# First mixer: the whole convolution on VectorE, its normalized half multiplied into the output before the recurrence's half

## The chip, the cores and the metric

The kernel runs on one core of one Trainium2 chip. The core has TensorE (matrix products; PE in a profile), VectorE (DVE), ScalarE (ACT), GpSimd (POOL) and the DMA queues, most of whose transfers SyncE (SP) issues. The metric is device time in microseconds (us) of one execution, lower is better; three runs of the kernel before gave 2468.09, 2470.43 and 2472.05 us.

## The reference, cut to what matters

Two transformer blocks of 512 tokens and width 1024 run one after the other; the change is in the first mixer of the first block:

```python
h = x @ w_in                                   # 512 x 3072
q, f_pre, i_v, g, a, a_gate = split(h)         # each 512 x 512
f = lb + (1 - lb) * sigmoid(f_pre); k = (1 - lb) * sigmoid(-f_pre)
o = hgrn2_chunked(q, k, i_v, log(f))           # S_t = diag(f_t) S_{t-1} + k_t v_t^T, chunks of 32
o = o * rsqrt(mean(o * o) + eps)               # per head of 128
o = o * hg_norm_g * silu(g)
u = a * sigmoid(a_gate)
u = conv_causal(u, cv_w, 31 taps, per channel) + cv_b
u = silu(layer_norm(u, cv_ln_g, cv_ln_b))
y = concatenate([o, u]) @ w_out                # rows 0..511 of w_out meet o, 512..1023 meet u
x = layer_norm(ALPHA * x + y)                  # goes on into the cross attention
```

Everything is float32.

## The kernel before, in words

A float32 product is made of three TensorE products of split operands: `split` (L152, L153) writes a rounded high part with ScalarE and the remainder with VectorE, and `mm3` (L180 to L182) multiplies high by high, high by low and low by high. Weights come in units of two k-slices of 128 rows (`chunk`): a DMA into a ring of 5 buffers `raw`, then the two split instructions into a ring of 4 buffers `w` (the second half of an output projection, `wb`, has buffers of its own). A unit can be split only when the products of the unit four places earlier have been done.

The mixer makes, in the order of its code: the gate and the value of the convolution (`u`, with channels on partitions, four groups f of 128 channels by 512 tokens); the forget gate and `v`; the convolution (`conv`, L674 to L686: 31 lags, each one instruction per channel group, which adds a shifted copy of `u` times a tap to `acc`); the cumulative sums of the gates (`cums`); the product for q; keys and values of the coming cross attention from the memory (`kv_k`, `kv_v`); the recurrence (`recur`, four turns t of 128 tokens: `advance` transposes q and k (L415), multiplies them (L731), masks (L734), makes the state increments of four chunks (L742) and adds them up on VectorE (L749); `readout` multiplies them out head by head (L766, L769) and normalizes); the product for g; the transposes of the recurrence's result into `yT`; and the output projection `lin_out`, which runs the four k-slices of the recurrence's half first, then `conv_norm` (the convolution's transposes L556, its normalization and transposes into the other half of `yT`), then the rest.

Of the four channel groups of the convolution, three are VectorE's. For the fourth, each lag is an activation on ScalarE (L683, `u` times the tap into one buffer `conv`) and an addition on GpSimd (L684).

The framework sets the order: it simulates the program and writes one fixed list of instructions for each engine, by priorities which follow the order of the code, except that weight units are pulled ahead (`high_priority`, `ahead`) and that the convolution is pushed back by 3000 (`later`). So an instruction of each engine waits behind all that stand before it in its list, whether it needs them or not.

Of the kernel before, what the change touches and what calls it, by code (L numbers as in the profile page):

```python
# [13 lines left out]
AF = mybir.ActivationFunctionType  # L14
ALU = mybir.AluOpType
# [57 lines left out]
class Net:  # L73
# [284 lines left out]
        out(1, 0, x)  # L358
        yield

    def lin_out(self, xT, W, first, norm, nxt, k0=0, nk=8, between=None, aside=None):
        split = 4 if between else 0
        ua = self.chunk(W, 0, 512, k0, nk)
        ps = [None] * 4
        if between:
            for t in range(4):
                ps[t] = self.bank([128, 512])
                self.mm_b(ps[t:t + 1], [t], xT, ua, range(split), nk)
            between()
        ub = self.chunk(W, 512, 512, k0, nk, big=True)  # L370
        if aside:
            aside()
        nxt = nxt()
        nxt, early = nxt if isinstance(nxt, tuple) else (nxt, None)
        ev = self.tail(512, first, norm, nxt)
        for half, t in ((0, 0), (0, 1), (1, 0), (1, 1), (0, 2), (0, 3), (1, 2), (1, 3)):
            if half == 0:
                p = ps[t] or self.bank([128, 512])
                self.mm_b([p], [t], xT, ua, range(split, nk), nk)
                self.resid(t, p, 0, first)  # L380
                if early:
                    early(t)
            else:
                p = self.bank([128, 512])
                self.mm_b([p], [t], xT, ub, range(nk), nk)
                ev(t, p)

    def mm_b(self, ps, tiles, xT, units, ks, nk):
        for k in ks:
            u = units[k // 2]  # L390
            xh, xl = xT(k)
            for i, t in enumerate(tiles):
                tk = slice(t * 128, t * 128 + 128)
                self.mm3(ps[i], xh[:, tk], xl[:, tk], u[:, 0, k % 2], u[:, 1, k % 2], k == 0, k == nk - 1)

    def lin_b(self, xT, W, c0, evac, w=512, k0=0, nk=8, groups=((0, 1, 2, 3),), **kw):
        units = self.chunk(W, c0, w, k0, nk, **kw)
# [61 lines left out]
    def hgrn_mixer(self):  # L459
        nc, a = self.nc, self.a  # L460
        W = a["ab_w_in"][0]
        hi, lo = self.new_xT()
        for t in range(4):
            for half in range(2):
                self.to_T(self.r[t][:, half * 512:half * 512 + 512], hi, lo, t, half)
        xT = self.pair_view(hi, lo)

        pack1 = self.slot([128, 4, 512], name="pack1")
        pack2 = self.slot([128, 4, 512], name="pack2")
        lb, om, hg, cg = (pack1[:, i, :] for i in range(4))  # L470
        cb = pack2[:, 2, :]
        cw, cwT = pack2[:, 3, 0:128], pack2[:, 3, 128:256]
        nc.gpsimd.dma_start(cw[0:124, :], a["cv_w"][0, :, 0, :].rearrange("j (c p) -> (j c) p", p=128))
        nc.gpsimd.dma_start(cw[124:128, :], a["cv_b"][0].rearrange("(c p) -> c p", p=128))
        cps = self.xbank([128, 128])
        nc.tensor.transpose(cps, cw, self.ident)
        nc.scalar.activation(cwT, cps, AF.Copy)

        u = self.slot([128, 4, 512], name="u")
        acc = self.slot([128, 4, 512], name="acc")  # L480

        def ev_gate(f, ps, t0, t1):
            nc.scalar.activation(u[:, f, t0:t1], ps, AF.Sigmoid)

        def ev_a(f, ps, t0, t1):
            nc.vector.tensor_tensor(u[:, f, t0:t1], u[:, f, t0:t1], ps, ALU.mult)

        self.lin_a(xT, W, 2560, ev_gate, halves=True, units=self.first)
        self.lin_a(xT, W, 2048, ev_a)
        mT = self.mem_T(0)  # L490

        lbr = self.slot([128, 3, 512], name="lbr")
        nc.gpsimd.dma_start(lbr, a["lb_param"].unsqueeze(0).broadcast_to([128, 3, 512]))
        nc.vector.tensor_tensor(om, lbr[:, 0], lbr[:, 1], ALU.max)
        nc.vector.tensor_tensor(om, om, lbr[:, 2], ALU.max)
        for i in range(3):
            nc.vector.tensor_tensor(lbr[:, i], lbr[:, i], om, ALU.subtract)
        nc.scalar.activation(lbr, lbr, AF.Exp)
        nc.vector.tensor_tensor(om, lbr[:, 0], lbr[:, 1], ALU.add)
        nc.vector.tensor_tensor(om, om, lbr[:, 2], ALU.add)  # L500
        nc.vector.reciprocal(om, om)
        nc.vector.tensor_tensor(lb, lbr[:, 0], om, ALU.mult)
        nc.vector.tensor_scalar(om, lb, -1.0, 1.0, ALU.mult, ALU.add)

        lf = self.slot([128, 4, 512], name="lf")
        kt = self.slot([128, 4, 512], name="kt")
        ke = self.slot([128, 4, 512], name="ke")

        def ev_f(t, ps):
            nc.scalar.activation(lf[:, t], ps, AF.Sigmoid)  # L510
            nc.scalar.activation(kt[:, t], ps, AF.Sigmoid, scale=-1.0)
            nc.vector.tensor_tensor(lf[:, t], lf[:, t], om, ALU.mult)
            nc.vector.tensor_tensor(lf[:, t], lf[:, t], lb, ALU.add)
            nc.vector.tensor_tensor(kt[:, t], kt[:, t], om, ALU.mult)

        self.lin_b(xT, W, 512, ev_f)
        v = self.slot([128, 4, 512], name="v")
        self.lin_b(xT, W, 1024, lambda t, ps: nc.scalar.activation(v[:, t], ps, AF.Copy))
        nc.scalar.activation(lf, lf, AF.Ln)

        with self.later(3000):
            self.conv(u, acc, cwT)

        qt = self.slot([128, 4, 512], name="qt")
        dec = pack2[:, 3, 256:320].rearrange("p (t h c) -> p t h c", t=4, h=4)
        for t in range(4):
            self.cums(t, lf[:, t], kt[:, t], ke[:, t], qt[:, t], dec[:, t], TRI, REV, 32)

        self.lin_b(xT, W, 0, lambda t, ps: nc.vector.tensor_tensor(qt[:, t], qt[:, t], ps, ALU.mult))
        self.kv_k(0, mT)  # L530
        self.kv_v(0, mT)
        g = self.slot([128, 4, 512], name="g")
        self.bload(hg, a["hg_norm_g"][0])

        def ev_g(t, ps):
            nc.scalar.activation(g[:, t], ps, AF.Silu)
            nc.gpsimd.tensor_tensor(g[:, t], g[:, t], hg, ALU.mult)

        self.masked = [pack2[:, i, :].rearrange("p (h t) -> p h t", h=4) for i in range(2)]
        nc.gpsimd.memset(pack2[:, 0:2, :], 0.0)  # L540
        col = lambda x: lambda t, h: x[:, t, h * 128:h * 128 + 128]
        self.recur(qt, kt, ke, col(v), dec, TRI, 32, 128, col(qt))
        self.lin_b(xT, W, 1536, ev_g, ahead=700)
        yh, yl = self.new_xT("yT")
        for t in range(4):
            nc.gpsimd.tensor_tensor(qt[:, t], qt[:, t], g[:, t], ALU.mult)
            self.to_T(qt[:, t, :], yh, yl, t, 0)

        self.bload(cg, a["cv_ln_g"][0])
        self.bload(cb, a["cv_ln_b"][0])  # L550

        def conv_norm():
            for t in range(4):
                ps = self.xbank([128, 4, 128])
                for f in range(4):
                    nc.tensor.transpose(ps[:, f, :], acc[:, f, t * 128:t * 128 + 128], self.ident)  # L556
                pf = ps.rearrange("p a b -> p (a b)")
                mv, rs = self.ln_stats([pf])
                cu = self.tmp()
                nc.vector.scalar_tensor_tensor(cu, pf, mv[:, 0:1], cg, ALU.subtract, ALU.mult)  # L560
                nc.vector.scalar_tensor_tensor(cu, cu, rs[:, 0:1], cb, ALU.mult, ALU.add)
                nc.scalar.activation(cu, cu, AF.Silu)
                self.to_T(cu, yh, yl, t, 1)

        lg, lb_ = self.gains("ln_mix", 0)
        yT = self.pair_view(yh, yl)
        Wo = a["ab_w_out"][0]
        self.lin_out(yT, Wo, True, (lg, lb_), self.next_split, between=conv_norm)

    def gains(self, name, l):  # L570
        return self.bcast(self.a[name + "_g"][l], "w4k", 1024), self.bcast(self.a[name + "_b"][l], "w4k", 1024)
# [100 lines left out]
    def conv(self, u, acc, cwT):  # L672
        nc = self.nc
        for lag in range(31):  # L674
            for f in range(4):
                col = cwT[:, 4 * (30 - lag) + f:4 * (30 - lag) + f + 1]
                bias = cwT[:, 124 + f:125 + f]
                src, dst = u[:, f, :512 - lag], acc[:, f, lag:]
                if lag == 0:
                    (nc.gpsimd if f == 3 else nc.vector).tensor_scalar(dst, src, col, bias, ALU.mult, ALU.add)  # L680
                elif f == 3:
                    p = self.wt([128, 512], "conv", bufs=1)[:, lag:]
                    nc.scalar.activation(p, src, AF.Identity, scale=col)  # L683
                    nc.gpsimd.tensor_tensor(dst, dst, p, ALU.add)  # L684
                else:
                    nc.vector.scalar_tensor_tensor(dst, src, col, dst, ALU.mult, ALU.add)  # L686

# [611 lines left out]
```

## Time and profile before

| what | value |
|---|---|
| median of 3 runs | 2470.43 us (2468.09 to 2472.05) |
| the profiled execution | 2471.44 us, of which the span 2469.6 us |
| PE busy | 2414.4 us (98%) |
| DVE busy | 1509.4 us (61%) |
| ACT busy | 1024.4 us (41%) |
| POOL busy | 180.5 us (7%) |
| mean granted clock of TensorE | 0.989 of full speed |

Busy time is the union of an engine's instructions. TensorE's is a rough measure, since its products overlap and since the same products take twice as long at half the clock. The mixer fills the first 321 us of the span. Times in the rows are counted from the span's start.

### The profile page before, as it was taken

How to read it: one execution, taken by the hardware profiler on the slowest of the kernel's cores; microseconds unless marked ns; L12 is line 12 of the kernel's file. 1: busy time of each engine (PE TensorE's matmuls, PEld its weight loads, DVE VectorE, ACT ScalarE, POOL GpSimd, SP SyncE). 2: the span in 40 equal slices, each digit the busy share in tenths (PEclk: the TensorE clock that was granted, in tenths of full speed). 3: DMA queues.
4: the chain of work that ended last, by engine and by line, in shares of the span. 5: the costliest groups of instructions: out<-in, count | busy, mean ns of one | idle time of the engine just before them, and what ended most of it. 6: DMA issues, size and time to landing. Idle time of an engine off the chain costs nothing.

```text
span 2469.6 us, 30360 instructions
## 1 busy us (share of the span) xinstructions
PE 2414.4 (98%) x12094; PEld 2010.3 (81%) x12094; DVE 1509.4 (61%) x1994; ACT 1024.4 (41%) x1620; POOL 180.5 (7%) x219
## 2 busy tenths in 40 slices
PE   8989999999999999999999999999999999999998
PEld 8877787888888997888888786888888877888887
DVE  4799475555566766455566423466876467487674
ACT  3653343233333343233334633534444456444443
POOL 1151200000000000000002003200000100000000
PEclk9999899999999999999999999999999999999999
DMA  6333122235344342334434123235553411144452
GB/s 234 103 103 111 54 83 81 84 112 171 109 143 153 126 133 77 94 132 141 141 124 132 60 86 42 87 111 171 179 172 119 161 62 52 60 171 150 155 173 77
DMA packets 148990, 291.92 MB, mean 118 GB/s; under 512 B 9449, under 2 KB 15909, under 8 KB 148592
## 3 DMA queue, kind: packets, MB, share of 16 engines
q1 hardware_dynamic: 146176, 282.17, 34.4%
q0 software_dynamic: 2096, 6.76, 1.4%
q8 instruction: 95, 1.56, 0.2%
q10 hardware_dynamic: 576, 1.05, 0.1%
q14 instruction: 47, 0.39, 0.0%
HBM read 286.77 MB, written 6.32 MB: 119 GB/s over the span
## 4 chain that ended last, share of the span: by engine, by line
PE 88%; DVE 7%; ACT 2%; issue 1%; DMA 1%; POOL 0%; SPq 0%; POOLq 0%; DVEq 0%; ACTq 0%
PE mm L180 23%; PE mm L181 23%; PE mm L182 23%; PE aux L182 5%; PE aux L180 4%; PE aux L181 4%; DVE acc L686 2%; PE aux L415 2%; PE aux L742 1%; DVE w L153 1%; PE mm L769 1%; PE mm L766 1%; PE aux L1219 0%; DVE bn L436 0%; ACT A L152 0%
## 5 line engine op out<-in xcount | busy, mean ns | idle before, releaser
L181 PE MATMUL mm<-xTl,w 128*128 128x512 f32 (+1 forms) x1696 | 614.3, 363 | 2.2 <-DVE xTl L153 2.2
L180 PE MATMUL mm<-xTh,w 128*128 128x512 f32 (+1 forms) x1696 | 611.4, 363 | 2.8 <-ACT w L172 1.8
L182 PE MATMUL mm<-xTh,w 128*128 128x512 f32 (+1 forms) x1696 | 574.0, 362 | 0.0
L153 DVE TENSOR_TENSOR w<-raw,w 128x1024 fp32r<-128x1024 f32 (+1 forms) x286 | 340.4, 1195 | 349.2 <-ACT w L152 348.9
L152 ACT ACTIVATE w<-raw 128x1024 fp32r<-128x1024 f32 (+1 forms) x286 | 293.6, 1030 | 579.4 <-PE mm L182 460.3
L180 PEld LDWEIGHTS mm<-xTh,w 128*128 128x128 f32 x1696 | 320.5, 190 | 53.2 <-ACT w L172 2.6
L181 PEld LDWEIGHTS mm<-xTl,w 128*128 128x128 f32 x1696 | 321.6, 190 | 50.9 <-DVE xTl L153 2.4
L182 PEld LDWEIGHTS mm<-xTh,w 128*128 128x128 f32 x1696 | 320.4, 190 | 48.8
L173 DVE SCALAR_TENSOR_TENSOR w<-raw,gains_T,w 128x512 fp32r<-128x512 f32 (+1 forms) x200 | 140.7, 736 | 122.1 <-ACT w L172 121.6
L172 ACT ACTIVATE w<-raw,gains_T 128x512 fp32r<-128x512 f32 (+1 forms) x200 | 131.1, 707 | 149.0 <-PE mm L182 141.6
L180 PE MATMUL aux<-w,A 128*128 128x512 f32 x440 | 169.6, 391 | 2.1 <-ACT A L152 2.1
L181 PE MATMUL aux<-w,A 128*128 128x512 f32 x440 | 171.4, 390 | 0.0
L182 PE MATMUL aux<-w,A 128*128 128x512 f32 x440 | 170.1, 391 | 1.1 <-DVE A L153 0.7
L181 PE MATMUL mm<-w,xTh 128*128 128x512 f32 (+1 forms) x352 | 135.1, 384 | 0.0
L182 PE MATMUL mm<-w,xTl 128*128 128x512 f32 (+1 forms) x352 | 134.6, 385 | 0.0
L180 PE MATMUL mm<-w,xTh 128*128 128x512 f32 (+1 forms) x352 | 134.6, 385 | 0.0
L152 ACT ACTIVATE w<-chain 128x1024 fp32r<-128x1024 f32 x60 | 63.8, 1063 | 133.4 <-DVE chain L305 52.5
L180 PEld LDWEIGHTS aux<-w,A 128*128 128x128 f32 x440 | 82.6, 188 | 22.7 <-ACT A L152 5.8
L182 PEld LDWEIGHTS aux<-w,A 128*128 128x128 f32 x440 | 82.6, 188 | 21.0 <-DVE A L153 4.1
L181 PEld LDWEIGHTS aux<-w,A 128*128 128x128 f32 x440 | 82.6, 188 | 16.9
L455 DVE TENSOR_TENSOR r<-r,mm 128x512 f32<-128x512 f32 x76 | 51.4, 682 | 55.8 <-PE mm L182 55.8
L153 DVE TENSOR_TENSOR xTl<-aux,xTh 128x512 fp32r<-128x512 f32 x72 | 47.3, 682 | 60.1 <-ACT xTh L152 60.1
(358 smaller groups left out, 4186.9 us busy)
## 6 DMA issues: line engine op xcount, KB each, us to landing
raw<-in_w_down SPq DMA_DIRECT2D x124, 512.0 KB, 3.6
raw<-in_ffn_wd SPq DMA_DIRECT2D x84, 512.0 KB, 3.4
raw<-in_w_up SPq DMA_DIRECT2D x64, 512.0 KB, 4.6
raw<-in_ffn_wg SPq DMA_DIRECT2D x40, 512.0 KB, 3.8
raw<-in_ffn_wu SPq DMA_DIRECT2D x40, 512.0 KB, 3.6
raw<-in_ab_w_in SPq DMA_DIRECT2D x24, 512.0 KB, 4.2
raw<-in_a_w_in SPq DMA_DIRECT2D x24, 512.0 KB, 3.6
raw<-in_xa_wk SPq DMA_DIRECT2D x16, 512.0 KB, 3.4
```

The source lines that it names most:

```text
L152: self.nc.scalar.activation(hi, src, AF.Copy)
L153: self.nc.vector.tensor_tensor(lo, src, hi.bitcast(F32), ALU.subtract)
L172: nc.scalar.activation(u[:, 0, i], raw[:, i], AF.Identity, scale=g)
L173: nc.vector.scalar_tensor_tensor(u[:, 1, i], raw[:, i], g, u[:, 0, i].bitcast(F32), ALU.mult, ALU.subtract)
L180: nc.tensor.matmul(ps, lh, rh, start=start, stop=False, **kw)
L181: nc.tensor.matmul(ps, lh, rl, start=False, stop=False, **kw)
L182: nc.tensor.matmul(ps, ll, rh, start=False, stop=stop, **kw)
L415: self.nc.tensor.transpose(ps[:, j, :], src[:, j * 128:j * 128 + 128], self.ident)
L455: self.nc.vector.tensor_tensor(r, r, ps, op)
L686: nc.vector.scalar_tensor_tensor(dst, src, col, dst, ALU.mult, ALU.add)
L742: nc.tensor.matmul(d[:, h - h0, :], ke[rows, t, h * 128:h * 128 + 128], vh(t, h)[rows, :], start=True, stop=True)
L766: nc.tensor.matmul(o, P[:, h, :], vh(t, h), start=True, stop=False)
```

## The change

The convolution's fourth channel group goes to VectorE as the others, with the instruction that these use; ScalarE's and GpSimd's 30 instructions each (L683, L684) are gone. The product for g stands ahead of the recurrence, and so does the whole of the convolution's normalization with its transposes. A new function `out_start` begins the first half of the columns of the output projection with the four k-slices of the convolution (4 to 7), after the recurrence in the code; `lin_out` then adds the recurrence's slices (0 to 3) to the same banks. `between` is no longer used here (the cross attention still uses it). Nothing else in the program is changed.

```diff
+    def out_start(self, xT, W):
+        units = self.chunk(W, 0, 512, 4, 4)
+        ps = [self.bank([128, 512]) for _ in range(4)]
+        for t in range(4):
+            self.mm_b(ps[t:t + 1], [t], xT, [None] * 2 + units, range(4, 8), 8, 4, 3)
+        return ps
+
-    def lin_out(self, xT, W, first, norm, nxt, k0=0, nk=8, between=None, aside=None):
+    def lin_out(self, xT, W, first, norm, nxt, k0=0, nk=8, ps=None, between=None, aside=None):
         split = 4 if between else 0
-        ua = self.chunk(W, 0, 512, k0, nk)
-        ps = [None] * 4
+        k_first, k_last = (4, 3) if ps else (0, nk - 1)
+        ua = self.chunk(W, 0, 512, k0, 4 if ps else nk)
+        ps = ps or [None] * 4
...
-                self.mm_b([p], [t], xT, ua, range(split, nk), nk)
+                self.mm_b([p], [t], xT, ua, range(split, k_last + 1), nk, k_first, k_last)
...
+        self.lin_b(xT, W, 1536, ev_g, ahead=700)
+        yh, yl = self.new_xT("yT")
+        yT = self.pair_view(yh, yl)
+        Wo = a["ab_w_out"][0]
+        self.bload(cg, a["cv_ln_g"][0])
+        self.bload(cb, a["cv_ln_b"][0])
+        for t in range(4):
+            ps = self.xbank([128, 4, 128])
...
+            self.to_T(cu, yh, yl, t, 1)
         self.masked = [pack2[:, i, :].rearrange("p (h t) -> p h t", h=4) for i in range(2)]
         nc.gpsimd.memset(pack2[:, 0:2, :], 0.0)
         col = lambda x: lambda t, h: x[:, t, h * 128:h * 128 + 128]
         self.recur(qt, kt, ke, col(v), dec, TRI, 32, 128, col(qt))
-        self.lin_b(xT, W, 1536, ev_g, ahead=700)
-        yh, yl = self.new_xT("yT")
+        ps = self.out_start(yT, Wo)
+
         for t in range(4):
             nc.gpsimd.tensor_tensor(qt[:, t], qt[:, t], g[:, t], ALU.mult)
             self.to_T(qt[:, t, :], yh, yl, t, 0)
...
-        self.lin_out(yT, Wo, True, (lg, lb_), self.next_split, between=conv_norm)
+        self.lin_out(yT, Wo, True, (lg, lb_), self.next_split, ps=ps)
...
                 if lag == 0:
-                    (nc.gpsimd if f == 3 else nc.vector).tensor_scalar(dst, src, col, bias, ALU.mult, ALU.add)
-                elif f == 3:
-                    p = self.wt([128, 512], "conv", bufs=1)[:, lag:]
-                    nc.scalar.activation(p, src, AF.Identity, scale=col)
-                    nc.gpsimd.tensor_tensor(dst, dst, p, ALU.add)
+                    nc.vector.tensor_scalar(dst, src, col, cwT[:, 124 + f:125 + f], ALU.mult, ALU.add)
                 else:
                     nc.vector.scalar_tensor_tensor(dst, src, col, dst, ALU.mult, ALU.add)
```

First place: VectorE at the end of the convolution (`acc`), in the kernel before; `S` is the recurrence's state, `w` a weight unit.

```order
L686 SCALAR_TENSOR_TENSOR acc_182<-u_181,pack_22_175,acc_182 128x485 x3
L734 COPY_PREDICATED pack_22_175<-consts,aux_1715 128x512
L749 SCALAR_TENSOR_TENSOR S_1721<-S_1664,pack_22_175,aux_1722 128x128 x4
L686 SCALAR_TENSOR_TENSOR acc_182<-u_181,pack_22_175,acc_182 128x484 x3
L749 SCALAR_TENSOR_TENSOR S_1721<-S_1721,pack_22_175,aux_1731 128x128 x4
L686 SCALAR_TENSOR_TENSOR acc_182<-u_181,pack_22_175,acc_182 128x483 x2
L153 TENSOR_TENSOR w_2188<-raw_2186,w_2188 128x1024
```

The same place in the changed kernel; `bn`, `mv` and `tmp` belong to the convolution's normalization, `yTl` is the low part of its half of `yT`.

```order
L690 SCALAR_TENSOR_TENSOR acc_182<-u_181,pack_22_175,acc_182 128x483 x4
L690 SCALAR_TENSOR_TENSOR acc_182<-u_181,pack_22_175,acc_182 128x482 x4
L446 BN_STATS bn_1721<-aux_1716 128x6
L448 BN_AGGR mv_1723<-bn_1721 128x2
L562 SCALAR_TENSOR_TENSOR tmp_1728<-aux_1716,mv_1723,pack_21_174 128x512
L563 SCALAR_TENSOR_TENSOR tmp_1728<-tmp_1728,rs_1725,pack_22_175 128x512
L153 TENSOR_TENSOR yTl_1713<-aux_1732,yTh_1711 128x4x128
L446 BN_STATS bn_1744<-aux_1739 128x6
```

The state's additions no longer stand between lags: all 124 instructions of the convolution come first, then the four turns of the normalization one after the other, each with its last subtraction before the next one's statistics, and only then the first mask and state of the recurrence.

Second place: TensorE in the middle of the recurrence, in the kernel before; `mm_2026` and `mm_2029` are banks of the product for g, `mm_1643` the readout's bank.

```order
L182 MATMUL mm_2029<-w_2023,xTl_117 128x512
L180 MATMUL mm_2026<-w_2023,xTh_115 128x512
L742 MATMUL aux_1740<-v_727,ke_586 128x128 x4
L742 MATMUL aux_1749<-v_727,ke_586 128x128 x4
L766 MATMUL mm_1643<-v_727,pack_22_175 128x128
L415 MATMUL aux_1793<-consts,qt_1037 128x128 x4
L769 MATMUL mm_1643<-S_1664,tmp_1706 32x128
```

TensorE in the changed kernel, from the last product for g (`mm_1605`) to the first of the recurrence.

```order
L182 MATMUL mm_1605<-w_1599,xTl_117 128x512
L558 MATMUL aux_1716<-consts,acc_182 128x128 x4
L425 MATMUL aux_1732<-consts,tmp_1728 128x128 x4
L558 MATMUL aux_1739<-consts,acc_182 128x128 x4
L425 MATMUL aux_1755<-consts,tmp_1751 128x128 x4
L558 MATMUL aux_1762<-consts,acc_182 128x128 x4
L425 MATMUL aux_1778<-consts,tmp_1774 128x128 x4
L558 MATMUL aux_1785<-consts,acc_182 128x128 x4
L425 MATMUL aux_1801<-consts,tmp_1797 128x128 x4
L425 MATMUL aux_1810<-consts,qt_977 128x128 x4
L425 MATMUL aux_1817<-consts,kt_585 128x128 x4
L735 MATMUL aux_1824<-tmp_1815,tmp_1822 128x128 x4
```

The products for g no longer lie between those of the recurrence. Behind the last of them stand the convolution's eight groups of transposes, and the recurrence behind these.

Third place: TensorE in the changed kernel inside the recurrence; `mm_2182` is the output's bank of token tile 0, `w_2174` and `w_2179` the units of `out_start`.

```order
L773 MATMUL mm_1809<-S_1830,tmp_1815 32x128 x3
L180 MATMUL mm_2182<-w_2174,yTh_1711 128x512
L181 MATMUL mm_2182<-w_2174,yTh_1711 128x512
L182 MATMUL mm_2182<-w_2174,yTl_1713 128x512
L180 MATMUL mm_2182<-w_2179,yTh_1711 128x512
L181 MATMUL mm_2182<-w_2179,yTh_1711 128x512
L735 MATMUL aux_1881<-tmp_1872,tmp_1879 128x128 x4
L746 MATMUL aux_1888<-v_727,ke_586 128x128 x4
```

Between the recurrence's products now lie the 48 of `out_start` (in groups of 3, 5, 11, 6, 13 and 10), where the kernel before had the 96 of g and some of the memory's values.

## Rows read from the trace of the kernel before

**Rows 1.** The page: share of the chain that ended last, by engine.

```profile
PE 88%; DVE 7%; ACT 2%; issue 1%; DMA 1%; POOL 0%; SPq 0%; POOLq 0%; DVEq 0%; ACTq 0%
```

**Rows 2.** Stretches of the mixer: start:end and length, busy time by engine, clock, DMA.

```profile
226.00:232.00 6.00, 6.00 (x28) 4.88 (x26) 6.00 (x15) 2.20 (x5) 0.22 (x1) 1.00 0.22 81
145.50:203.00 57.50, 52.43 (x310) 45.07 (x310) 57.50 (x56) 31.00 (x45) 26.71 (x17) 0.95 0.37 121
203.00:242.00 39.00, 39.00 (x247) 29.18 (x246) 36.38 (x71) 10.86 (x27) 3.11 (x2) 1.00 0.34 111
246.30:266.60 20.30, 20.19 (x125) 14.00 (x124) 6.17 (x22) 7.77 (x23) 10.46 (x10) 0.51 0.03 8
```

**Rows 3.** Waits of TensorE from 100 to 200 us: total, times, longest.

```profile
PE mm L181 <- DVE w L153: 5.1, 5, 1.7
PE aux L696 <- DVE pack L706: 3.4, 1, 3.4
PE mm L180 <- DVE qt L529: 3.1, 1, 3.1
```

**Rows 4.** VectorE, groups of lines from 104 to 237.8 us: busy, mean ns.

```profile
L686 DVE SCALAR_TENSOR_TENSOR acc<-u,pack,acc 128x511 f32<-128x511 f32 (+29 forms) x90 | 83.3, 967 | 0.0
```

**Rows 5.** Timeline of VectorE: start us, us, engine, line, operation.

```profile
104.17 1.45 DVE L680 TENSOR_SCALAR acc<-u,pack 128x512 f32<-128x512 f32 x3
105.54 2.73 DVE L686 SCALAR_TENSOR_TENSOR acc<-u,pack,acc 128x511 f32<-128x511 f32 x4
108.18 1.22 DVE L153 TENSOR_TENSOR w<-raw,w 128x1024 fp32r<-128x1024 f32 x1
109.32 1.78 DVE L686 SCALAR_TENSOR_TENSOR acc<-u,pack,acc 128x510 f32<-128x510 f32 x1
...
219.00 4.53 DVE L686 SCALAR_TENSOR_TENSOR acc<-u,pack,acc 128x488 f32<-128x488 f32 x7
```

**Rows 6.** Timeline of GpSimd.

```profile
108.86 1.69 POOL L684 TENSOR_TENSOR acc<-acc,conv 128x510 f32<-128x510 f32 x1 [38.74 <-ACT conv L683]
...
257.18 4.93 POOL L537 TENSOR_TENSOR g<-g,pack 128x512 f32<-128x512 f32 x4
```

**Rows 7.** Timeline of one normalization turn of the convolution, VectorE and ScalarE.

```profile
275.66 0.70 DVE L436 BATCH_NORM_STATS2 bn<-aux 128x6 f32<-128x512 f32 x1 [2.33 <-PE aux L556]
276.27 0.67 DVE L153 TENSOR_TENSOR yTl<-aux,yTh 128x512 fp32r<-128x512 f32 x1
278.04 0.75 DVE L561 SCALAR_TENSOR_TENSOR tmp<-tmp,rs,pack 128x512 f32<-128x512 f32 x1 [0.22 <-POOL rs L430]
278.83 0.63 ACT L562 ACTIVATE tmp<-tmp 128x512 f32<-128x512 f32 x1 [3.01 <-DVE tmp L561]
```

**Rows 8.** Timeline of TensorE, fourth turn of the recurrence, clock 0.5.

```profile
251.57 1.12 PE L415 MATMUL aux<-consts,kt 128*128 128x128 f32 x4
255.38 5.36 PE L742 MATMUL aux<-v,ke 32*128 32x128 f32 x32
265.92 1.59 PE L415 MATMUL aux<-consts,qt 128*128 128x128 f32 x8
```

**Rows 9.** Timeline of TensorE, turns at full clock.

```profile
237.75 0.60 PE L415 MATMUL aux<-consts,kt 128*128 128x128 f32 x4
240.16 0.49 PE L766 MATMUL mm<-v,pack 128*128 128x128 f32 x2
240.93 1.16 PE L731 MATMUL aux<-tmp,tmp 128*128 128x128 f32 x8
242.02 3.52 PE L742 MATMUL aux<-v,ke 32*128 32x128 f32 x32
```

**Rows 10.** Timeline of TensorE at the seam to the attention.

```profile
321.01 0.74 PE L180 MATMUL mm<-xTh,w 128*128 128x256 f32 x4 [0.25 <-ACT xTh L152]
323.93 0.38 PE L181 MATMUL mm<-xTl,w 128*128 128x256 f32 x1 [2.17 <-DVE xTl L153]
```

More of the change, by code (lines that the diff above doesn't have):

```diff
@@ L386, in lin_out, with mm_b @@
                 ev(t, p)
-    def mm_b(self, ps, tiles, xT, units, ks, nk):
+    def mm_b(self, ps, tiles, xT, units, ks, nk, k_first=0, k_last=None):
+        k_last = nk - 1 if k_last is None else k_last
         for k in ks:
@@ L393, in mm_b @@
                 tk = slice(t * 128, t * 128 + 128)
-                self.mm3(ps[i], xh[:, tk], xl[:, tk], u[:, 0, k % 2], u[:, 1, k % 2], k == 0, k == nk - 1)
+                self.mm3(ps[i], xh[:, tk], xl[:, tk], u[:, 0, k % 2], u[:, 1, k % 2], k == k_first, k == k_last)
     def lin_b(self, xT, W, c0, evac, w=512, k0=0, nk=8, groups=((0, 1, 2, 3),), **kw):
@@ L537, in ev_g @@
             nc.gpsimd.tensor_tensor(g[:, t], g[:, t], hg, ALU.mult)
+        self.lin_b(xT, W, 1536, ev_g, ahead=700)
[6 more added lines that the diff above has]
+            ps = self.xbank([128, 4, 128])
+            for f in range(4):
+                nc.tensor.transpose(ps[:, f, :], acc[:, f, t * 128:t * 128 + 128], self.ident)
+            pf = ps.rearrange("p a b -> p (a b)")
+            mv, rs = self.ln_stats([pf])
+            cu = self.tmp()
+            nc.vector.scalar_tensor_tensor(cu, pf, mv[:, 0:1], cg, ALU.subtract, ALU.mult)
+            nc.vector.scalar_tensor_tensor(cu, cu, rs[:, 0:1], cb, ALU.mult, ALU.add)
+            nc.scalar.activation(cu, cu, AF.Silu)
+            self.to_T(cu, yh, yl, t, 1)
         self.masked = [pack2[:, i, :].rearrange("p (h t) -> p h t", h=4) for i in range(2)]
@@ L547, in hgrn_mixer @@
             self.to_T(qt[:, t, :], yh, yl, t, 0)
[L549 to L563, printed above, removed]
         lg, lb_ = self.gains("ln_mix", 0)
-        yT = self.pair_view(yh, yl)
-        Wo = a["ab_w_out"][0]
-        self.lin_out(yT, Wo, True, (lg, lb_), self.next_split, between=conv_norm)
+        self.lin_out(yT, Wo, True, (lg, lb_), self.next_split, ps=ps)
     def gains(self, name, l):
@@ L676, in conv @@
                 col = cwT[:, 4 * (30 - lag) + f:4 * (30 - lag) + f + 1]
-                bias = cwT[:, 124 + f:125 + f]
                 src, dst = u[:, f, :512 - lag], acc[:, f, lag:]
                 if lag == 0:
-                    (nc.gpsimd if f == 3 else nc.vector).tensor_scalar(dst, src, col, bias, ALU.mult, ALU.add)
-                elif f == 3:
-                    p = self.wt([128, 512], "conv", bufs=1)[:, lag:]
-                    nc.scalar.activation(p, src, AF.Identity, scale=col)
-                    nc.gpsimd.tensor_tensor(dst, dst, p, ALU.add)
+                    nc.vector.tensor_scalar(dst, src, col, cwT[:, 124 + f:125 + f], ALU.mult, ALU.add)
                 else:
```

## The prediction

> **What bounds the kernel now.** I read the chain of waits first: it lies on TensorE for 88% of the span and on VectorE for 7% [rows 1], so time is lost or won where TensorE waits or runs at half its clock. Then the stretches of the first mixer, the only part whose lists of instructions change. Without waits TensorE issues 28 products of 512 columns in 6.0 us [rows 2]; two of the 28 lie partly outside, so one takes some 0.23 us. From 100 to 200 us it waits 11.6 us, each time for VectorE [rows 3]. VectorE is busy without a gap from 145.5 to 203 us [rows 2]. Its convolution lines come every 0.65 us where GpSimd rests (seven in 4.53 us) and can take 1.78 us while GpSimd adds [rows 5, 6]; over 90 of them the mean is 0.967 us [rows 4]. From 203 to 242 us TensorE is full at full clock, since the products for g fill the gaps of the recurrence. In the recurrence's last 20.3 us, without such filling, the granted clock is 0.51, that is 1.2 instead of 2.4 GHz [rows 2].
>
> My mark for the end of the mixer is the first query product of the cross attention, at 321.0 us; it then stands 2.2 us for a remainder on VectorE and goes on at 323.9 us [rows 10]. From there the lists are the same, and TensorE is the bound, so I carry a shift of this mark to the end one for one.
>
> **The convolution.** Removed are 30 activations and 30 additions on ScalarE and GpSimd, and GpSimd's first lag; added are 31 lines on VectorE, 31 x 0.65 = 20 us. Removed with the additions is what they cost VectorE: 90 x (0.967 - 0.65) = 28 us of durations, of which about 0.07 us each is overlap with the next line, so 22 us in these lines, and a few more in the others. For VectorE this is about even, but the lines no longer stretch the first part. In the changed list its work from the start of the convolution at 104.2 us [rows 5] to the last lag is 4 first lags x 0.48 = 1.9, 120 lines x 0.65 = 78.0, 25 remainders of weight units x 1.14 = 28.5 (108.18 to 109.32 [rows 5]) and 15 other operations on 512 columns x 0.67 = 10 us (one such is in [rows 7]): 118.4 us, so the last lag ends at 222.6 us if VectorE never waits. It does wait: the last unit that it splits before the last 32 lines takes the buffer of the last unit of g. The memory's values ended at 203 us in the kernel before. Without the 11.6 us of waits, some 4 us at half clock behind the two long ones, and 5 us of the recurrence's products in between, that is 182 us; 96 products for g at 0.23 make it 204. ScalarE then evaluates g and rounds the unit (4 us), VectorE subtracts (1.1 us), and 32 lines x 0.65 = 21 us follow: 230 us. GpSimd's four multiplications by the norm gain (4.93 us together [rows 6]) meet these lines and may cost up to 4 x 1.1 us. I take 230 us, bounds 222.6 and 234.
>
> Here two rules of the Trainium skill stand against each other. "Perfetto Trace Analysis", section "Optimizing Scalar/DVE Operations", advises offloading to ScalarE or even GpSimd when VectorE is saturated, as it is here; by that alone this change is wrong: VectorE's lags, which ended at 237 us with 7 us of state work between them, would end at about 250 us, and the total would come some 20 us later than by my sum. "SBUF — State Buffer", section "Who interferes with whom", says that a VectorE instruction with two SBUF inputs and a GpSimd instruction that reads SBUF fully block each other; the lines of 1.78 us beside an addition of 1.69 us agree, so I count VectorE's part as even.
>
> **The convolution's normalization.** Before, it lay under the output's products. Now TensorE has nothing else in its list: from 204 us it waits for the last lag. A turn is serial: statistics to the second scaled addition 2.38 us less one subtraction of 0.59 that stood in between = 1.8; that addition 0.75; Silu 0.63 [rows 7]; four transposes at half clock 1.1 [rows 8] (0.6 at full [rows 9]); rounding 0.6; subtraction 0.67. Four turns of 5.5 us, plus 1.0 for the first transposes, less 1.3 because the recurrence's transposes only need the last Silu's: 21.7 us (19 at full clock). The recurrence begins at 252 us; before, its first products were spread from 157 us on.
>
> **The recurrence.** At half clock the last turn took 14.35 us from its transposes of k [rows 8], with those of q 15.2. At full clock: transposes 0.7, scores 1.1, state 3.5 (VectorE's additions, 4.2, lie beside it), four heads of 0.77: 8.4 us, from the starts and durations in [rows 9]. The 48 products between cost 11 us at full clock and 21 at half. So 4 x 8.4 + 11 = 45 us to 4 x 15.2 + 21 = 82 us. It begins after more than 40 us of nearly idle TensorE, so the first turn is at half clock; the filling is half as many products as before and none lies in the last turn. I take two turns at either clock and 13 us of filling: 60 us, nearer to the full clock, because the second and third turn have 22 and 23 products in them, as the lists show. It ends at 312 us.
>
> **The rest of the output.** 192 of its products stood behind the recurrence before; now 144 do: 33 us, plus 2 us for the first transposes and their split and 3 us for the others: 38 us. The mark comes at 350 us. The normalization of the convolution no longer shares VectorE with that of the residual, so I set it against 323.9 us: +26; about 1 us of clock at the seam comes back. The weights' DMAs only change places in SP's list by a few and are idle most of this time (DMA share 0.34 and less from 203 us on [rows 2]): nothing.
>
> **The sum.** 2471.4 us of the profiled execution + 25 = 2496.4; the median of the runs is 1.0 us lower, so 2495 us: slower by 1.0%. With all lower bounds (222.6, 19, 45, 36) the mark is at 323 us, 2470; with all upper ones (234, 22, 82, 39) at 377 us, 2523.
>
> **The rivals.**
> 1. Not slower: GpSimd's additions were the whole brake, and the change takes them away. VectorE reaches the last lag at 223 us, TensorE gets back its 11.6 us of waits and the clock lost behind them, and the 48 products hold the recurrence at full clock: the mark is at 323 us, 2470 us. For it: all waits of [rows 3] are on VectorE, and 203 to 242 us at clock 1.00 with such filling. Against: the unit that waits for g's last product, and a TensorE without work for 20 us before. It decides if both the last lag ends by 225 us and no turn is at half clock. A gain of some 6 us would need products for the gaps that the list does not have.
> 2. Cold throughout: the filling never lifts the clock, as the readouts did not from 246 to 266 us. Then 82 us for the recurrence: 2471.4 + 46, about 2516 us. Against: 22 products in a row of the second turn take several us, and the clock came back within the first such stretch behind the waits before.
> 3. The change doesn't do what it says (no output products between): the lists show all 48, so no chance of its own.
>
> **How the numbers follow.** My forecast, with 2480 to 2507 as its own range, 0.73; the first rival 0.10; the second 0.17. The range is 2476 to 2515: it leaves out most of the first rival and the upper bounds. 0.2%, 5 us, is what a measurement can tell. Slower: the forecast and the second rival, 0.90. Within 0.2%: 0.07, and faster 0.03, both from the first.
>
> **What will show it.** Right: convolution lines all at about 0.65 us until 225 to 234 us, with no wait of TensorE for VectorE's copies or q before 145 us; a hole on TensorE from about 204 us for over 20 us, then four short groups of transposes some 5.5 us apart; granted clock 0.5 there and in the first turn; the recurrence ending near 312 us; the mark near 349. Wrong: a last lag before 222 us or after 240, a recurrence shorter than 45 us, or a shift of the mark that is not found again in the total.

## The result, and the profile after

The changed kernel takes 2493.1 us (median of four runs, 2489.6 to 2494.9), the kernel before 2470.9 us on the same chips: ratio 1.0090, 95% interval 1.0077 to 1.0103. It is 0.9% slower; 2495 us was forecast, 2476 to 2515 the range. The profiled execution took 2489.59 us (span 2487.8 us), 18.2 us more than that of before.

The chain of waits of the changed kernel by engine, answering to [rows 1]; two points have gone from VectorE to TensorE, which says little, because the change sits in a tenth of the span (102 to 345 us):

```profile
PE 90%; DVE 5%; ACT 3%; issue 1%; DMA 1%; POOL 0%; SPq 0%; POOLq 0%; DVEq 0%; ACTq 0%
```

The stretches of the first mixer in the changed kernel, columns as in [rows 2] (start:end and length, busy time of TensorE, its weight loads, VectorE, ScalarE and GpSimd, clock, DMA share):

```profile
95.00:199.50 104.50, 103.51 (x554) 89.18 (x552) 100.24 (x138) 49.62 (x65) 1.27 (x1) 1.00 0.42 136
199.50:224.60 25.10, 0.05 (x1) 0.00 (x0) 25.10 (x35) 1.54 (x3) 4.99 (x4) 0.58 0.06 21
224.60:248.60 24.00, 8.68 (x32) 6.31 (x33) 13.20 (x22) 4.31 (x7) 3.13 (x8) 0.50 0.00 0
248.60:268.50 19.90, 19.16 (x91) 13.81 (x89) 5.58 (x18) 2.98 (x5) 0.00 (x0) 0.50 0.01 2
268.50:309.40 40.90, 40.79 (x332) 30.60 (x324) 20.20 (x56) 16.16 (x48) 8.06 (x10) 1.00 0.12 43
309.40:353.00 43.60, 43.60 (x240) 37.62 (x238) 32.34 (x42) 10.61 (x26) 10.86 (x11) 1.00 0.28 95
```

Read the second column against the length. Until 199.5 us TensorE is now full, where [rows 3] had 11.6 us of waits. Then it does nothing for 25.1 us while VectorE is busy for all 25.1, and in the next 24.0 us it has 8.7 us of work. What follows, 19.9 us at clock 0.50, is the first turn of the recurrence with three products of the output in it. The two stretches of waiting, 199 to 356 us, by line (total, times, longest):

```profile
PE aux L558 <- DVE acc L690: 25.6, 4, 25.1
PE aux L425 <- ACT tmp L564: 14.8, 4, 3.8
```

VectorE in the changed kernel (start, duration, line): the last lines of the convolution, which answer to [rows 5], and one turn of its normalization, which answers to [rows 7]:

```profile
181.52 4.59 DVE L690 SCALAR_TENSOR_TENSOR acc<-u,pack,acc 128x495 f32<-128x495 f32 x7
196.38 8.63 DVE L690 SCALAR_TENSOR_TENSOR acc<-u,pack,acc 128x491 f32<-128x491 f32 x7
206.07 20.40 DVE L690 SCALAR_TENSOR_TENSOR acc<-u,pack,acc 128x489 f32<-128x489 f32 x32
232.81 0.69 DVE L446 BATCH_NORM_STATS2 bn<-aux 128x6 f32<-128x512 f32 x1
234.69 0.75 DVE L563 SCALAR_TENSOR_TENSOR tmp<-tmp,rs,pack 128x512 f32<-128x512 f32 x1 [0.20 <-POOL rs L440]
237.94 0.69 DVE L153 TENSOR_TENSOR yTl<-aux,yTh 128x512 fp32r<-128x512 f32 x1 [2.50 <-ACT yTh L152]
```

The last lag ends at 226.5 us, and between the second addition of a turn and its last subtraction VectorE stands 2.5 us too: the turn is a chain through four engines, with nobody else in it. The seven lines at 196.38 us run beside the four multiplications that GpSimd makes from 198.23 to 204.48 us, and take 8.63 us instead of 4.59:

```profile
198.23 6.25 POOL L547 TENSOR_TENSOR g<-g,pack 128x512 f32<-128x512 f32 x4 [155.06 <-ACT g L546]
```

TensorE at the seams of the recurrence, at the scores of its second and fourth turn and at the mark, answering to [rows 8 to 10]:

```profile
248.63 1.06 PE L425 MATMUL aux<-consts,qt 128*128 128x128 f32 x4
268.59 0.49 PE L770 MATMUL mm<-v,pack 128*128 128x128 f32 x2
270.63 1.05 PE L735 MATMUL aux<-tmp,tmp 128*128 128x128 f32 x8
299.97 1.16 PE L735 MATMUL aux<-tmp,tmp 128*128 128x128 f32 x8
301.06 3.52 PE L746 MATMUL aux<-v,ke 32*128 32x128 f32 x32
309.37 0.47 PE L180 MATMUL mm<-w,yTh 128*128 128x512 f32 x1
344.47 0.64 PE L180 MATMUL mm<-xTh,w 128*128 128x256 f32 x4
344.94 0.28 PE L181 MATMUL mm<-xTl,w 128*128 128x256 f32 x1
```

The recurrence runs from 248.6 to 309.4 us. The query product that came at 323.93 us before [rows 10] comes at 344.94 us, 21.0 us later. Two corrections tie this to the total. The first line of the convolution started at 101.89 us here and at 104.17 us before [rows 5], though the instructions up to there are the same: 2.3 us that belong to the run (in e5, e8 and e9, which begin alike, that line starts at 101.97, 103.42 and 104.39 us), so the mixer itself became 23.3 us longer. And from the mark to the end the changed kernel needs 2.8 us less (2487.8 - 344.94 against 2469.6 - 323.93). Of these, 1.6 us come at the seam, where TensorE goes into the attention at full clock (1.00 in the first 6 us behind the mark, 0.72 before): the remainder of one weight unit that starts at 380.98 us before starts at 400.42 us, 19.4 us later. The other 1.2 us come and go in the rest of the span, where the code is the same. So -2.3 + 23.3 - 2.8 = 18.2 us, the whole difference of the two profiled executions. The medians differ by 22.2 us; the 4 us between stand in neither trace.

### The profile page after: what moved, and what is told of

Its sections match the earlier page's. It is cut to its first block, busy times and chain, and to the rows that moved or that the text cites. A ratio compares the mean times of both kernels' runs of the same rounds, so it can differ in the third digit from the quotient of the medians.

```text
span 2487.8 us, 30332 instructions
## 1 busy us (share of the span) xinstructions
PE 2410.0 (97%) x12094; PEld 2009.2 (81%) x12094; DVE 1510.0 (61%) x2025; ACT 1006.4 (40%) x1590; POOL 133.1 (5%) x188
## 4 chain that ended last, share of the span: by engine, by line
PE 90%; DVE 5%; ACT 3%; issue 1%; DMA 1%; POOL 0%; SPq 0%; POOLq 0%; DVEq 0%; ACTq 0%
PE mm L180 23%; PE mm L181 23%; PE mm L182 23%; PE aux L182 4%; PE aux L180 4%; PE aux L181 4%; PE aux L425 2%; DVE acc L690 1%; PE aux L746 1%; PE mm L773 1%; PE mm L770 1%; DMA raw<-in_ffn_wd 1%; DVE w L153 1%; PE aux L1223 0%; DVE A L153 0%
## 5 line engine op out<-in xcount | busy, mean ns | idle before, releaser
L180 PEld LDWEIGHTS aux<-w,A 128*128 128x128 f32 x440 | 82.6, 188 | 22.2 <-ACT A L152 5.5
L690 DVE SCALAR_TENSOR_TENSOR acc<-u,pack,acc 128x511 f32<-128x511 f32 (+29 forms) x120 | 85.0, 765 | 0.0
```

The lines of the kernel that those rows point to most:

```text
L180: nc.tensor.matmul(ps, lh, rh, start=start, stop=False, **kw)
```

## The experiments

My theory: the loss is the order. TensorE's other work is used up at 199.5 us, and the recurrence waits for the last lag and the serial normalization; the convolution's move to VectorE is a small gain by itself. The rival: 31 lines more on a VectorE that had no gap are the loss. Ratios are to the kernel before on the same chip.

**e1: the convolution alone.** In the kernel before:

```diff
-                bias = cwT[:, 124 + f:125 + f]
...
-                    (nc.gpsimd if f == 3 else nc.vector).tensor_scalar(dst, src, col, bias, ALU.mult, ALU.add)
-                elif f == 3:
-                    p = self.wt([128, 512], "conv", bufs=1)[:, lag:]
-                    nc.scalar.activation(p, src, AF.Identity, scale=col)
-                    nc.gpsimd.tensor_tensor(dst, dst, p, ALU.add)
+                    nc.vector.tensor_scalar(dst, src, col, cwT[:, 124 + f:125 + f], ALU.mult, ALU.add)
```

> The kernel before with one edit alone: the convolution's fourth channel group on VectorE, the order of the parts as before (recurrence, product for g, the recurrence's half of the output, normalization of the convolution, the other half). My theory is that the loss of the change comes from the new order (TensorE stands from the end of g to the last lag and through four serial normalization turns, and the recurrence begins cold), not from the convolution's move. Then the waits of TensorE for VectorE between 100 and 200 us (11.6 us) and some 4 us at half clock behind them go, and the recurrence, whose state additions stand between the lags, ends at about the same time after them: 9 us faster than before, about 2462 us, between 2456 and 2472. The rival, that 20 us more of lags on a VectorE that is busy without a gap are the loss themselves: 10 to 20 us slower than before, 2480 to 2490.

Measured: 2463.9 us, ratio 0.9986 (0.9976 to 0.9996): faster, by 3.5 us (the medians differ by 5.5), where 9 were expected. That is less than the 0.2% which the prediction took for the least that a measurement can tell, but the interval leaves out 1, and a loss of 10 to 20 us is ruled out. The convolution's lines of e1, then of before with the order changed alone (e2, below); the columns are those of [rows 4]:

```profile
L681 DVE SCALAR_TENSOR_TENSOR acc<-u,pack,acc 128x511 f32<-128x511 f32 (+29 forms) x120 | 81.5, 727 | 0.0
```

```profile
L695 DVE SCALAR_TENSOR_TENSOR acc<-u,pack,acc 128x511 f32<-128x511 f32 (+29 forms) x90 | 86.1, 1003 | 0.0
```

120 lines take less VectorE time than 90 beside GpSimd's additions. From 100 to 200 us TensorE of e1 has no wait at all, and its last product for g ends at 215.8 us, 22 us earlier than before (20 counted from the first line of the convolution). Of this little is left: from that line to the first query product the mixer takes 210.3 us, 216.8 before. The next stretch of e1 shows why:

```profile
230.00:257.00 27.00, 24.48 (x113) 18.19 (x114) 18.56 (x46) 9.46 (x26) 10.90 (x11) 0.51 0.02 6
```

The last two turns of the recurrence have lost their filling earlier and run at half clock for 27 us instead of 20.3 [rows 2].

**e2: the order alone.** The changed kernel with the fourth channel group back on ScalarE and GpSimd (the old `conv`).

> The changed kernel with the convolution's fourth group back on ScalarE and GpSimd: the new order alone. My theory: the waits between 100 and 200 us come back, VectorE's 90 lines are stretched by GpSimd's additions again (mean near 0.97 us), the last lag comes at about 230 us instead of 226 and all behind it later by as much: 4 us slower than the changed kernel, about 2497, between 2490 and 2505. The rival (31 lines fewer on VectorE bring the last lag 20 us forward): 2473 us.

Measured: 2494.3 us, ratio 1.0108 (1.0090 to 1.0127), in the range expected and not clear of the changed kernel. The order costs 1.1% without the convolution's move. TensorE's hole is shorter here, 11.7 us, because the waits of [rows 3] are back and g ends later; the last lag comes at 233.8 us. The two halves add up: +1.08 - 0.14 = +0.94% against +0.90% for both. The rival falls.

**e3: the normalization in stages.** All four tiles' statistics, scaling and Silu first:

```diff
-            cu = self.tmp()
+            cu = u[:, t]
...
-            self.to_T(cu, yh, yl, t, 1)
+        for t in range(4):
+            self.to_T(u[:, t], yh, yl, t, 1)
```

> The changed kernel with the convolution's normalization written in two loops: statistics, scaling and Silu of all four token tiles first (into the buffer of u), then the four groups of transposes. If the serial turns of 5.75 us stand on the path, the first transposes of the recurrence come 8 us earlier (about 240.5 instead of 248.6 us) and the whole is 8 us shorter than the changed kernel, about 2485, between 2481 and 2490. If the recurrence waited for something else by then, no change: 2493.

Measured: 2480.6 us, ratio 1.0048 (1.0031 to 1.0065), below the changed kernel by 0.42%, 10 us. The recurrence's first transposes:

```profile
239.81 1.06 PE L425 MATMUL aux<-consts,qt 128*128 128x128 f32 x4
```

They come 8.8 us earlier than at 248.63, and 10.7 us earlier counted from the first line of the convolution, which began at 103.8 us here. The serial turns stood on the path; 8 us were expected, and the median lies just under the range of 2481 to 2490. The clock does not account for it: here it was at 1.00 from 242 to 279 us and at 0.51 behind that, and the recurrence takes 62.3 us up to the first product of the output behind it (302.10 us), in the changed kernel 60.7.

**e4: TensorE kept busy.** In the changed kernel:

```diff
+        warm = self.bank([128, 512])
+        for i in range(96):
+            nc.tensor.matmul(warm, hi[0][:, 0, 0:128], hi[0][:, i % 4, :], start=True, stop=True)
...
+            if t < 3:
+                for i in range(8):
+                    nc.tensor.matmul(warm, yh[1][:, i % 4, t * 128:t * 128 + 128], hi[0][:, i % 4, :], start=True, stop=True)
```

> The changed kernel with 120 extra products on TensorE whose results nothing reads: 96 in the hole behind the last product for g, and 8 behind each of the first three turns of the convolution's normalization, where TensorE waits some 3.8 us. If the half clock of the first turn of the recurrence (19.9 us at 0.50) and of the transposes before it comes from the empty TensorE ahead of it, these run at 1.00: the first turn takes about 10 us less, a transposes group 0.5 less, and the whole is 10 to 12 us shorter in spite of more work: about 2482, between 2478 and 2487. If the recurrence's small products are at half clock for what they are, nothing is won: 2493 to 2498.

Measured: 2484.8 us, ratio 1.0078 (1.0058 to 1.0098), below the changed kernel by 3 us by the ratios and by 8 us by the medians; the two intervals overlap, so a gain in the total is not shown. What the trace shows is the clock. Its stretches, from the first transposes of the normalization on:

```profile
226.50:245.50 19.00, 11.81 (x49) 8.24 (x50) 11.44 (x21) 3.68 (x6) 2.35 (x6) 0.76 0.00 0
248.60:258.00 9.40, 8.60 (x64) 6.71 (x62) 4.36 (x14) 1.58 (x3) 0.00 (x0) 1.00 0.01 3
258.00:296.90 38.90, 38.69 (x309) 28.85 (x308) 17.31 (x53) 13.42 (x44) 7.92 (x10) 1.00 0.13 45
296.90:304.00 7.10, 7.10 (x45) 4.38 (x43) 6.30 (x10) 5.62 (x9) 0.16 (x1) 0.52 0.28 85
```

```profile
248.60 0.60 PE L425 MATMUL aux<-consts,qt 128*128 128x128 f32 x4
263.88 1.05 PE L741 MATMUL aux<-tmp,tmp 128*128 128x128 f32 x8
```

From the recurrence's first transposes to the scores of its second turn it takes 15.3 us; in the changed kernel 22.0 us, to 270.63. And 15 products of the output lie in these 15.3 us, only 8 in the 22.0: 7 x 0.23 = 1.6 us more work. The recurrence's products are at 0.50 behind an idle TensorE and at 1.00 behind a busy one: the cold start costs 8.3 us, and 2 us more in the normalization's transposes, 10.3 us together, where 10 to 12 were expected. Some of it is lost again, since here the last readouts fell to 0.52: from the first line of the convolution to the first query product the mixer takes 235.5 us, 7.1 us less than in the changed kernel (242.6).

**e6: half of the lags.** The changed kernel with `for lag in range(16)`, which leaves out the last 15 lags.

> The changed kernel without the last 15 of the 31 lags (60 of 124 lines left out). If the last lag sets the start of the normalization, and by its serial turns that of the recurrence, both come when the last product for g allows it: the hole of 25 us on TensorE shrinks to under 5 us, the recurrence begins near 224 us instead of 248.6, and the whole takes about 2469 us (2464 to 2475). If TensorE's hole had another cause (the weights of the next unit, the gates), it stays and the time is near 2490.

Measured: 2470.7 us, ratio 0.9994 (0.9978 to 1.0011); 2469 was expected. TensorE's only large wait is now the normalization's, and the recurrence begins 23.3 us earlier:

```profile
PE aux L425 <- ACT tmp L564: 18.3, 4, 6.9
```

```profile
225.31 1.06 PE L425 MATMUL aux<-consts,qt 128*128 128x128 f32 x4
```

The last lag set the start of all that follows. Even so the kernel is only level with the one before; the serial normalization (18.3 us of waits) and a first turn at half clock are still in it.

**e7: no output products between.** The changed kernel without `out_start` (and `ps=ps`).

> The changed kernel without out_start: nothing of the output between the recurrence's products, all 192 products of the output's first half behind it. If it is these 48 products that bring the clock back in the second turn, the recurrence stays at 0.5 throughout: four turns of 15.2 us, 61 us, as long as with the filling; then 48 products more behind it, 11 us: about 2504 us (2499 to 2510). If the clock comes back without them after about 20 us, the recurrence takes 45 us and the time is about 2488 us (2484 to 2493).

Measured: 2486.0 us, ratio 1.0068 (1.0045 to 1.0091): the second of the two forecasts. My theory of the clock fell: without a single product of 512 columns on TensorE from 199.5 to 299.6 us, the clock came back. Its stretches:

```profile
249.00:264.00 15.00, 14.25 (x68) 11.25 (x69) 5.58 (x18) 2.39 (x4) 0.00 (x0) 0.50 0.01 2
264.00:272.90 8.90, 8.79 (x80) 6.32 (x78) 3.99 (x14) 3.21 (x13) 2.40 (x3) 0.88 0.16 60
272.90:275.30 2.40, 2.40 (x15) 1.43 (x13) 0.95 (x4) 0.60 (x1) 0.08 (x1) 0.50 0.04 7
275.30:292.70 17.40, 16.74 (x163) 12.70 (x162) 8.33 (x29) 6.90 (x27) 5.00 (x7) 0.99 0.03 8
292.70:302.50 9.80, 9.80 (x56) 6.36 (x56) 7.72 (x14) 6.54 (x12) 0.55 (x1) 0.50 0.39 121
```

It does not hold, though: it falls twice more, while in the changed kernel it stayed up. The recurrence takes 50.7 us here, where 45 were expected, from 248.96 us to the first product of the output at 299.62 us; with 48 x 0.23 = 11 us for the products that now come later that is 61.7 us, against 60.7 in the changed kernel. The products between gain nothing that can be measured: the intervals of the two kernels overlap, and e7 has the lower median.

**e5: seven lags behind the recurrence.** In e1, to see whether the lags between the state additions hold it:

```diff
+        cw2 = pack1[:, 0, 0:128]
+        nc.vector.scalar_tensor_tensor(cw2, qt[:, 2, 0:128], 0.0, cwT, ALU.mult, ALU.add)
+        with self.later(3000):
+            self.conv(u, acc, cw2, range(24, 31))
...
+    def conv(self, u, acc, cwT, lags=range(24)):
```

> The kernel of e1 (order of before, whole convolution on VectorE), with its last 7 lags (28 lines, 18 us) held back until the third turn of the recurrence has been read out: they take their taps from a copy that one VectorE line makes after it. In e1 the product for g ended 22 us earlier than before, but VectorE's lags, four between two groups of state additions, paced the last two turns, and TensorE was at 0.51 from 230 to 257 us. If the lags between the state additions hold the recurrence up there, its last readout comes 8 to 18 us earlier and the kernel takes about 2454 us (between 2446 and 2460, e1 had 2464). If the half clock alone makes these turns long, little is won: 2461 to 2466.

Measured: 2472.9 us, ratio 1.0015 (1.0002 to 1.0027): slower than e1, against both forecasts. The recurrence did end 12 us earlier (last readout 249.1 us, e1 261.2). But 7.6 us of this are only order: from 250.60 to 258.17 us e1 has twelve products of the output and eight transposes in front of its last readouts, which e5 has behind them. What was really won, some 4 us, was given back at once: behind the recurrence VectorE had the held lines in front of the remainder of the output's operand,

```profile
245.13 11.12 DVE L685 SCALAR_TENSOR_TENSOR acc<-u,pack,acc 128x488 f32<-128x488 f32 x11
256.18 0.68 DVE L153 TENSOR_TENSOR yTl<-aux,yTh 128x512 fp32r<-128x512 f32 x1
```

and TensorE waited for that remainder and then for the convolution's normalization, in e5's list of waits:

```profile
PE mm L182 <- DVE yTl L153: 4.4, 2, 3.9
PE aux L415 <- ACT tmp L566: 4.0, 1, 4.0
PE aux L560 <- DVE acc L685: 1.4, 1, 1.4
```

**e8: four lags behind it.** `range(27, 31)` in place of `range(24, 31)`.

> The kernel of e5 with only the last 4 lags (16 lines, 10.4 us) held back instead of 7. In e5 the recurrence ended 12 us earlier than in e1, but the 28 lines then stood before the first remainders of the output's operand and before the convolution's normalization, and TensorE waited for these. If this is where the gain went, 12 lines fewer bring the last lag from 271 to about 260 us, under the output's products, and the kernel takes about 2458 us (2452 to 2464; e1 2464, e5 2473). If the lines that go back between the state additions cost as much as they save, 2463 to 2470.

Measured: 2463.2 us, ratio 0.9976 (0.9966 to 0.9987), 9.8 us under e5, at the seam of the two forecasts, and not clear of e1. TensorE's wait for the remainder is as in e5:

```profile
PE mm L182 <- DVE yTl L153: 4.7, 2, 4.0
```

**e9: no multiplications on GpSimd.** In e8, `nc.gpsimd` becomes `nc.vector` for the two products with g.

> The kernel of e8 with the eight multiplications of 512 columns that GpSimd still had in this mixer (norm gain into g, g into the recurrence's result) on VectorE. In e8 12 lines of the convolution took 12.73 us beside them, where 12 alone take 7.8, and the first remainder of the output's operand stood behind these lines, so that TensorE waited 4.0 us for it. If the stretching comes from GpSimd's multiplications running beside VectorE's lines, these lines take 0.65 us each, the wait of 4.0 us goes to under 1 and the kernel takes about 2459 us (2455 to 2462; e8 had 2463). If the lines stretch for another reason, or VectorE's eight more instructions (5 us) cost what is won, 2462 to 2466.

Measured: 2462.3 us, ratio 0.9968 (0.9957 to 0.9979): between the two forecasts and not clear of e8, but the stretching is gone. The last lines of the convolution in e8, then in e9 (busy, mean ns):

```profile
L685 DVE SCALAR_TENSOR_TENSOR acc<-u,pack,acc 128x485 f32<-128x485 f32 (+3 forms) x16 | 15.4, 1025 | 0.0
```

```profile
L685 DVE SCALAR_TENSOR_TENSOR acc<-u,pack,acc 128x485 f32<-128x485 f32 (+3 forms) x16 | 10.6, 718 | 0.0
```

```profile
PE mm L182 <- DVE yTl L153: 0.7, 1, 0.7
```

The wait of 4.0 us is 0.7 us now. Why the total follows so little can be read in part: the gain was lost in the recurrence. The mask of its fourth turn comes at 244.43 us in e9 and at 239.50 in e8, 4.0 us later counted from the first line of the convolution (104.39 and 103.42 us), and up to the first query product the two mixers take 208.7 and 208.3 us. TensorE of e9 went to half clock at 222 us, that of e8 at 232 us; why, no run shows. (The profiled execution of e8 took 2470.7 us, more than its median, but the excess lies behind the mixer: 2154.3 us from the mark to the end, 2145.4 in e9.) e9 is the fastest version found: 0.3% under the kernel before, 1.2% under the changed one.

## Why the prediction was right, and where it was not

The sum came within 2 us of the median, and part of that is luck. It is counted in profiled executions, where 25 us more were forecast and 18.2 measured; at the mark 26 us were forecast and 23.3 measured, counted from the first line of the convolution. Two steps below failed, the wait in front of the last lag and the clock in the recurrence, and in each another error made up for most of it.

**The first part.** Right. The waits of [rows 3] went, and e1 shows that the convolution's move did it. The lines came at 0.65 us except beside GpSimd's four multiplications, which cost 4.0 us (8.63 - 4.59); 4.4 had been allowed. Of the two rules of the Trainium skill that were weighed, the one on interference ("SBUF — State Buffer", section "Who interferes with whom") is what the lines show here, 718 ns without and 1025 ns with GpSimd beside them in e9 and e8. The advice of the Trainium skill to offload a saturated VectorE ("Perfetto Trace Analysis", section "Optimizing Scalar/DVE Operations") gains nothing in this kernel, by e1's interval. The two are not opposed, as the prediction had it: that section goes on to say that offloading between VectorE and GpSimd might not help.

**The last lag.** 226.5 us instead of 230; 2.3 us of that is the earlier start. That everything behind waits for it was right (e6). What sets it was not: I had VectorE wait for the unit behind g's last product (199.5 us, 204 forecast). ScalarE had rounded that unit at 201.1 us, and VectorE came to its subtraction only at 204.93 us, behind its own lines and without a wait. The first row below is all that VectorE waited from 102 to 226 us (total, times, longest):

```profile
DVE w L153 <- ACT w L152: 2.3, 6, 1.0
200.08 1.05 ACT L152 ACTIVATE w<-raw 128x1024 fp32r<-128x1024 f32 x1
204.93 1.21 DVE L153 TENSOR_TENSOR w<-raw,w 128x1024 fp32r<-128x1024 f32 x1
```

So VectorE's own work set the last lag: 101.9 + the 118.4 us of work that I had taken for a bound + 2.3 of waits + 4.0 beside GpSimd = 226.6 us.

**The normalization.** Turns of 5.75 us, 5.5 forecast, at clock 0.50 as expected. The recurrence began at 248.6 us, 252 forecast, 250.9 by the time of before.

**The recurrence.** 60.7 us, 60 forecast, but for the wrong reason: this is the step that failed most. I had "two turns at either clock", since the 48 products would bring the clock back. It came back at 268.5 us, in the first turn's readouts, before the second turn's filling, and e7 shows that it comes without them; and it stayed for the last turn, which I had cold. With 1.2 cold turns (19.9 us, less some 1.7 for the three products of the output in it, of 15.2) instead of two the sum would have been some 6 us shorter, and the other error made up for most of it: a turn at full clock costs about 10 us, not 8.4. From the scores of the second turn (270.63 us) to those of the third (287.76) it took 17.1 us with 30 products of 0.23 between, so 10.2; to those of the fourth 12.2 us with 10, so 9.9. I had counted one of the two groups of transposes (0.66 us), and the state's products as one piece of 3.52 us, where cut by others they take 1.71 + 1.15 + 1.15 = 4.0 us; some 0.4 us I can't assign. Two errors nearly cancelled.

**The rest of the output.** 35.1 us from its first product behind the recurrence (309.37 us) to the first query product (344.47 us), 38 forecast: the 2 us for the first transposes and their split were not paid, since TensorE began the output right behind the transposes, without a wait. At the seam 1.6 us came back instead of 1; another 1.2 us came back further on.

**The rivals.** Not slower: its first condition, the last lag by 225 us, was missed by 1.5 us in the run's own time, but that alone decided nothing: in e6 all behind the last lag comes 23 us earlier, and the kernel is still not faster than before (0.9994). Its second condition failed clearly, with a first turn at half clock. Cold throughout: what TensorE did from 224.6 to 268.5 us ran at 0.50, and nothing in the recurrence behind that. What stays open is when the clock falls in the recurrence. The same readouts, without filling, ran at 1.00 for 16.8 us in the changed kernel (292.6 to 309.4 us), fell after 8.5 us in the kernel before (246.2 us), after 12.4 us in e4 (296.9 us), after 3 us in e3 (279.4 us) and twice in e7. No run here separates what differs.

## What to carry to other kernels

Moving work from GpSimd to a full VectorE can be free, when the two slow each other down; look at the durations beside each other's work before counting instructions. When independent products are moved in front of a serial chain, the chain loses its cover: ask what TensorE has left to do while the chain runs, and at what clock it will begin afterwards. Lines held back to free one wait stand in front of the next one: e5 brought the end of the recurrence 12 us forward, some 4 us of it real, and paid more behind it.

## What was not expected of the hardware

TensorE's clock rose from 0.50 to 1.00 in the middle of the recurrence's small products alone (e7, at about 265 us), with no product of 512 columns near it, and fell and rose again within the next 30 us. GpSimd's multiplication of 512 columns is slowed by VectorE's lines as they are by it: four took 6.25 us beside them in the changed kernel and 4.93 us before, when the convolution was over [rows 6].
